# First chunk of a two-layer encoder: raw weights with a place for each k-tile, token-major squares, 32-column float32 gates

## Chip, cores and metric

The kernel runs on one core of one Trainium2 chip. The metric is the device time of one execution in microseconds, as the median of several runs.

## What is computed

The reference is a two-layer encoder trunk on 256 tokens of width 2048, all in float32. Layer 0 mixes tokens with a bidirectional mLSTM (8 heads), layer 1 with a bidirectional gated recurrence (16 heads); each mixer and each gated MLP (width 5504) is preceded by an RMSNorm and added to the residual. Only the first projection concerns us:

```python
def rmsnorm(x, g):
    xf = x.astype(jnp.float32)
    xf = xf * lax.rsqrt(jnp.mean(xf * xf, axis=-1, keepdims=True) + EPS)
    return xf.astype(x.dtype) * g

def mlstm_mixer(hn, w_in, b_gate, head_g, w_out):
    p = hn @ w_in
    q, k, v, o, gates = jnp.split(p, [A_QK, 2 * A_QK, 2 * A_QK + A_V, 2 * A_QK + 2 * A_V], axis=-1)
    gates = (gates + b_gate).astype(jnp.float32).reshape(b, s, 4, A_HEADS)
    ...
```

There are 32 gate columns (4 kinds x 8 heads). `w_in` is 2048 x 6176, and about 440 MB of weights go through the core in one execution.

## The kernel before

**Products.** Weights and activations are each split into two parts of type float32r, a rounded high part and the rest: `wh` and `wl` for weights, the two halves of `xt` for x. A product is high by high plus the two mixed terms. ScalarE casts (`wh`, line 154, and `xt`, line 226), VectorE subtracts (`wl`, line 155, and `xt`, line 227). The activations are multiplied by the norm's gain `g` while they are split; the factor 1/rms of each token is multiplied in only when a product leaves PSUM, through `R` (a row for each token) or `rc` (a column).

**Chunks.** All projections form one list of chunks, each 256 or 512 output columns over all k-tiles of 128 rows. `stream` walks through it. A generator, `split_weights`, loads raw weights (SP's queue, line 138, three buffers `raw` of 2048 columns), splits them in pieces of 1024 columns into `wh` and `wl` (four buffers each), and is asked for pieces three ahead of their use. In a chunk of kind "fm" (features on partitions) a k-tile takes lines 202 and 206; in one of kind "tm" (tokens on partitions) lines 215 to 217, twice. Each chunk holds PSUM banks, of which there are four for products, until its `done` function has emptied them. Other work (heads, norms, transposes) is put between the matmuls by the `Side` object's estimates of time. The order of each engine's instructions is finally set by a scheduler with a simulated time line; an instruction that is pinned (`tc.keep_in_program_order`) stays behind the instruction of its engine that the program has before it.

**The first chunk** is of a kind of its own, "first". It makes 512 columns of v and, in a third PSUM bank, the gates: 32 gate columns spread over 128 by zeros, so that each k-tile has 640 columns. Beside the six v matmuls a k-tile has two for the gates (lines 219, 220). Its raw weights go through the three `raw` buffers, k-tiles 0 to 3 one by one and then in pairs (`FIRST`). x arrives feature-major as `xT`, in the tile `gx`, with the gains in its first 16 columns: k-tiles 0 and 1 on ScalarE's queue (line 143), the others on SP's, each behind the raw weights of its k-tile (line 146). In the loop ScalarE also squares four k-tiles of x at a time (line 258), VectorE adds these up (line 262), and `pc` (line 269) sums over the features. From that `finish` makes `rc` and, with the matmul `pr` (line 308), `R`. Constants and parameters are loaded behind the tenth k-tile (line 242).

After the chunk, x is loaded again, token-major, over the place of `gx` (`hm`, the residual; line 602, GpSimd's queue). `gates` then makes the mLSTM's decay terms from the gate products (lines 435 to 482), while the second chunk (`w_aq[0]`: q) runs. Ahead of it all, 39 small matmuls on a tile of ones (`idle`, line 880) keep TensorE busy during the first loads.

Of the kernel before, what the change touches and what calls it, by code (L numbers as in the profile page):

```python
# [8 lines left out]
F32 = mybir.dt.float32  # L9
F32R = mybir.dt.float32r  # L10
# [5 lines left out]
P = 128  # L16
T = 256
# [29 lines left out]
FIRST = (0, 1, 2, 3, 4, 6, 8, 10, 12, 14, 16)  # L47
# [4 lines left out]
C_ID, C_MF, C_MB, C_LV = 0, 128, 384, 640  # L52
# [3 lines left out]
def trunk_kernel(ctx, tc, xT, x_d, fg_d, pp_d, cst_d, w_first, w_aq, w_ak, w_av, w_ao, w_aout,  # L56
# [15 lines left out]
    gx = keep.tile([P, KT + KT * T], F32, name="gx")  # L72
    hx = gx[:, KT:].rearrange("p (k t) -> p k t", k=KT)
    hT = [hx[:, k] for k in range(KT)]
    hm = hx.rearrange("p k t -> p (k t)").rearrange("p (a c) -> p a c", a=2)
# [41 lines left out]
    class Chunk:  # L117
        def __init__(self, kind, src, nk, x, done, before=None, last=False, swap=()):
            self.last, self.swap = last, swap
            self.kind, self.src, self.nk, self.x, self.done, self.before = kind, src, nk, x, done, before  # L120
            self.width = {"fm": 256, "tm": 512, "first": 512 + P}[kind]

    def split_weights(chunks):

        first = True
        for ch in chunks:
            total = ch.nk * ch.width
            cuts = [0]
            if first:
                cuts = [k * ch.width for k in FIRST]  # L130
            while cuts[-1] < total:
                cuts.append(min(total, cuts[-1] + 2048))
            step = ch.width if first else 1024
            for b0, b1 in zip(cuts, cuts[1:]):
                n = b1 - b0
                raw = wpool.tile([P, 2048], F32, tag="raw", bufs=RAW, name="raw")
                pin = tc.keep_in_program_order if first else lambda ins: ins
                pin(nc.sync.dma_start(raw[:, :n], ch.src[:, b0:b0 + n]))
                if first:
                    k0, k1 = b0 // ch.width, b1 // ch.width  # L140
                    if k0 == 0:
                        for a, b in ((0, KT + T), (KT + T, KT + 2 * T)):
                            nc.scalar.dma_start(gx[:, a:b], xT[:, a:b])
                    elif k0 > 1:
                        a, b = KT + k0 * T, KT + k1 * T
                        pin(nc.sync.dma_start(gx[:, a:b], xT[:, a:b]))
                for c0 in range(0, n, step):
                    m = min(step, n - c0)
                    wh = wpool.tile([P, 1024], F32R, tag="wh", bufs=WB, name="wh")
                    wl = wpool.tile([P, 1024], F32R, tag="wl", bufs=WB, name="wl")  # L150
                    r = raw[:, c0:c0 + m]
                    if first and b0 == 0:
                        ch.x(0, pin)
                    pin(act.copy(wh[:, :m], r))  # L154
                    pin(dve.tensor_tensor(wl[:, :m], r, wh[:, :m].bitcast(F32), ALU.subtract))  # L155
                    if first and b0:
                        ch.x((b0 + c0) // ch.width, pin)
                    yield wh, wl, m // ch.width
            first = False

    def stream(chunks):
# [10 lines left out]
        for ch in chunks:  # L172
            if ch.before:
                ch.before()
            ps = [psm.tile([P, 512], F32, tag="mm", name="mm") for _ in range(3 if ch.kind == "first" else 2)]
            k = 0
            while k < ch.nk:
# [31 lines left out]
                for kk in range(n):  # L209
                    x = ch.x(k)  # L210
                    st, sp = k == 0, k == ch.nk - 1
                    c = slice(kk * 512, (kk + 1) * 512)
                    for t in range(2):
                        xh, xl = x[:, t * P:(t + 1) * P], x[:, T + t * P:T + (t + 1) * P]
                        pe.matmul(ps[t], xh, wh[:, c], start=st, stop=False)  # L215
                        pe.matmul(ps[t], xh, wl[:, c], start=False, stop=False)  # L216
                        pe.matmul(ps[t], xl, wh[:, c], start=False, stop=sp)  # L217
                    if ch.kind == "first":
                        pe.matmul(ps[2], wh[:, 512:512 + P], x, start=st, stop=False)
                        pe.matmul(ps[2][:, 0:T], wl[:, 512:512 + P], x[:, 0:T], start=False, stop=sp)  # L220
                    side.tick(1.3)
                    k += 1
# [22 lines left out]
    class Norm:  # L245
# [5 lines left out]
        def take(self, k, src, *pin):  # L251
            self.xs[k] = keep.tile([P, 2 * T], F32R, tag=f"xt{k}", name=f"xt{k}")
            split(self.xs[k], src, gx[:, k:k + 1] if pin else col(self.g, self.o + k), *pin)

        def squares(self, i, mp, pin):

            s = mp.tile([P, 4 * T], F32, tag="sq4", bufs=2, name="sq4")
            pin(act.activation(s, hx[:, 4 * i:4 * i + 4].rearrange("p a b -> p (a b)"), AF.Square))
            if i == 0:
                self.acc4 = s  # L260
                return
            pin(dve.tensor_tensor(self.acc4, self.acc4, s, ALU.add))
            if i == 3:
                a = self.acc4
                dve.tensor_tensor(a[:, 0:2 * T], a[:, 0:2 * T], a[:, 2 * T:4 * T], ALU.add)
                dve.tensor_tensor(a[:, 0:T], a[:, 0:T], a[:, T:2 * T], ALU.add)
                pc = [aux("pc") for _ in range(2)]
                for t in range(2):
                    pe.matmul(pc[t][:, 0:1], a[:, t * P:(t + 1) * P], ones[:, 0:1], start=True, stop=True)
                self.finish([pc[t][:, 0:1] for t in range(2)])  # L270

        def add(self, c):

            if c == 0:
                self.ss = ev.tile([P, 2, 4], F32, tag="ss8", bufs=2, name="ss8")
            cs = slice(512 * c, 512 * c + 512)
            for t in range(2):
                square(hm[:, t, cs], self.ss[:, t, c:c + 1])
            side.push(self.turn(c))

        def turn(self, c):
# [10 lines left out]
            if c == 3:  # L292
                ss = self.ss
                dve.tensor_tensor(ss[:, :, 0:2], ss[:, :, 0:2], ss[:, :, 2:4], ALU.add)
                dve.tensor_tensor(ss[:, :, 0:1], ss[:, :, 0:1], ss[:, :, 1:2], ALU.add)
                self.finish([ss[:, t, 0:1] for t in range(2)])

        def finish(self, sums):
# [75 lines left out]
    def square(src, total):  # L374
        jk = ev.tile([P, 512], F32, tag="jk", bufs=1, name="jk")
        act.activation(jk, src, AF.Square, accum_out=total)
# [27 lines left out]
    def mlstm(norm, nxt):  # L404
# [3 lines left out]
        cp = tc.tile_pool(name="cols", bufs=1)  # L408
        box = {}

        def first_x(k, pin=None):
            if pin is None:
                return norm.xs[k]
            norm.take(k, hT[k], pin)
            if k in (5, 9, 12, 15):
                if k == 5:
                    box["sp"] = startup.enter_context(tc.tile_pool(name="sp", bufs=1))
                norm.squares((5, 9, 12, 15).index(k), box["sp"], pin)
                if k == 15:
                    startup.close()  # L420
            if k == 10:
                late(cst[:, 0:C_LV], cst_d[:, 0:C_LV])
                late(pp, pp_d)

        def begin():
            c = stack.enter_context(cp)
# [142 lines left out]
        for pr in range(AH // 2):  # L569
# [27 lines left out]

            def done_first(ps, done_v=done_v):
                done_v(ps[0:2])
                gates(ps[2])  # L600
                for t in range(2):
                    pool.dma_start(hm[:, t], x_d[t])

            if pr == 0:
                chunks.append(Chunk("first", w_first, KT, first_x, done_first, begin))
            else:
                chunks.append(Chunk("tm", w_av[pr - 1], KT, norm.x, done_v))
# [270 lines left out]
    for i in range(39):  # L878
        o = i % 4 * QUAD
        pe.matmul(idle[o:o + QUAD, 0:120], ones[:, 0:QUAD], ones[:, 0:120], start=True, stop=True)  # L880
# [31 lines left out]
def _constants():  # L912
    c = np.zeros((P, NCST), np.float32)
    s, t = np.arange(P)[:, None], np.arange(P)[None, :]
    c[:, C_ID:C_ID + P] = s == t
    c[:, C_MF:C_MF + P] = np.where(s > t, BIG, 0.0)
# [7 lines left out]
def layout(x, norm_mix_g, norm_ffn_g, mlstm_w_in, mlstm_b_gate, mlstm_head_g, mlstm_w_out, hgrn_w_in, hgrn_lb,  # L924
# [3 lines left out]
    wg = np.zeros((D, P), np.float32)  # L928
    bg = np.zeros((P, 1), np.float32)
    for i, r in enumerate((0, 64, 32, 96)):  # L930
        wg[:, r:r + AH] = wa[:, 6144 + i * AH:6144 + (i + 1) * AH]
# [12 lines left out]
        w_first=np.concatenate([wa[:, 2048:2560].reshape(KT, P, 512), wg.reshape(KT, P, P)], axis=2)  # L944
        .transpose(1, 0, 2).reshape(P, KT * (512 + P)),
# [11 lines left out]
def build(nc, ins, out_shape=(2, P, D), **kw):  # L957
# [4 lines left out]
    with tile.TileContext(nc, schedule_with_timeline_sim=True) as tc:  # L962
        with ExitStack() as ctx:
            trunk_kernel(ctx, tc, ap["xT"], ap["x"], ap["fg"], ap["pp"], ap["cst"], ap["w_first"],
# [15 lines left out]
```

## Time and profile before

| | us |
|---|---|
| median of 3 runs (2418.76 to 2421.82) | 2419.44 |
| the profiled execution | 2421.37 |
| its span | 2419.6 |
| TensorE busy | 2406.7 |
| VectorE busy | 1694.1 |
| ScalarE busy | 1221.1 |

The profile is of one execution. The span is the time from its first to its last instruction; the profiled execution's own time has a little beside it. Busy times of an engine overlap those of the others, and matmuls are pipelined, so that the sum of their lengths says less than the distance between their starts. The granted TensorE clock was 0.999 over the span.

### The profile page before, as it was taken

How to read it: one execution, taken by the hardware profiler on the slowest of the kernel's cores; microseconds unless marked ns; L12 is line 12 of the kernel's file. 1: busy time of each engine (PE TensorE's matmuls, PEld its weight loads, DVE VectorE, ACT ScalarE, POOL GpSimd, SP SyncE). 2: the span in 40 equal slices, each digit the busy share in tenths (PEclk: the TensorE clock that was granted, in tenths of full speed). 3: DMA queues.
4: the chain of work that ended last, by engine and by line, in shares of the span. 5: the costliest groups of instructions: out<-in, count | busy, mean ns of one | idle time of the engine just before them, and what ended most of it. 6: DMA issues, size and time to landing. Idle time of an engine off the chain costs nothing.

```text
span 2419.6 us, 36956 instructions
## 1 busy us (share of the span) xinstructions
PE 2406.7 (99%) x14646; PEld 2060.3 (85%) x14646; DVE 1694.1 (70%) x2784; ACT 1221.1 (50%) x1879; POOL 161.7 (7%) x223
## 2 busy tenths in 40 slices
PE   9999999999999999999999999999999999999998
PEld 7888888888888888888888888888888888888887
DVE  7766656777645777656898989885777754677754
ACT  6655455444434445445555555555544443444443
POOL 0100000000000000001222222220000000000000
PEclk9999999999999999999999999999999999999999
DMA  8654555555555555555545554555555555555554
GB/s 290 200 182 162 186 176 189 190 188 189 181 196 201 188 187 189 192 185 183 173 173 175 175 175 167 168 185 190 183 191 190 192 188 195 194 190 192 192 188 142
DMA packets 66925, 451.90 MB, mean 187 GB/s; under 512 B 7600, under 2 KB 8368, under 8 KB 14144
## 3 DMA queue, kind: packets, MB, share of 16 engines
q1 hardware_dynamic: 64656, 442.92, 54.0%
q0 software_dynamic: 1232, 5.31, 0.9%
q8 instruction: 114, 1.87, 0.3%
q10 hardware_dynamic: 864, 1.32, 0.2%
q14 instruction: 59, 0.48, 0.1%
HBM read 447.35 MB, written 2.16 MB: 186 GB/s over the span
## 4 chain that ended last, share of the span: by engine, by line
PE 98%; DMA 1%; DVE 0%; issue 0%; ACT 0%; SPq 0%; POOLq 0%; POOL 0%; DVEq 0%
PE mm L202 36%; PE mm L206 18%; PE mm L215 13%; PE mm L216 13%; PE mm L217 13%; DMA gx<-in_xT 1%; PE pn L533 1%; PE py L763 1%; PE pd L713 0%; PE pz L288 0%; PE pa L713 0%; PE S L519 0%; PE pz L784 0%; PE pa L738 0%; PE pa L737 0%
## 5 line engine op out<-in xcount | busy, mean ns | idle before, releaser
L155 DVE TENSOR_TENSOR wl<-raw,wh 128x1024 fp32r<-128x1024 f32 (+1 forms) x848 | 1031.9, 1218 | 582.3 <-ACT wh L154 572.4
L202 PE MATMUL mm<-xt,wh 128*128 128x512 f32 x3776 | 1315.6, 394 | 0.0
L154 ACT CAST wh<-raw 128x1024 fp32r<-128x1024 f32 (+1 forms) x848 | 881.2, 1041 | 859.0 <-PE mm L217 400.9
L206 PE MATMUL mm<-xt,wl 128*128 128x256 f32 x3776 | 1048.8, 278 | 0.0
L202 PEld LDWEIGHTS mm<-xt,wh 128*128 128x128 f32 x3776 | 707.0, 188 | 160.7
L206 PEld LDWEIGHTS mm<-xt,wl 128*128 128x128 f32 x3776 | 710.0, 188 | 3.2 <-DVE wl L155 0.3
L217 PE MATMUL mm<-wh,g 128*128 128x512 f32 x674 | 262.8, 390 | 0.0
L215 PE MATMUL mm<-wh,g 128*128 128x512 f32 x674 | 262.5, 390 | 0.0
L216 PE MATMUL mm<-wl,g 128*128 128x512 f32 x674 | 262.3, 389 | 0.0
L215 PE MATMUL mm<-wh,xt 128*128 128x512 f32 x512 | 198.9, 393 | 2.9 <-ACT xt L226 2.1
L216 PE MATMUL mm<-wl,xt 128*128 128x512 f32 x512 | 198.5, 392 | 0.2 <-DVE wl L155 0.2
L217 PE MATMUL mm<-wh,xt 128*128 128x512 f32 x512 | 198.0, 391 | 0.0
L231 ACT COPY b<-mm 128x256 f32<-128x256 f32 x237 | 87.6, 369 | 166.6 <-PE mm L206 166.5
L217 PEld LDWEIGHTS mm<-wh,g 128*128 128x128 f32 x674 | 126.5, 188 | 26.5
L215 PEld LDWEIGHTS mm<-wh,g 128*128 128x128 f32 x674 | 126.5, 188 | 26.4
L216 PEld LDWEIGHTS mm<-wl,g 128*128 128x128 f32 x674 | 126.5, 188 | 25.8
L215 PEld LDWEIGHTS mm<-wh,xt 128*128 128x128 f32 x512 | 95.1, 188 | 23.2 <-ACT xt L226 3.3
L217 PEld LDWEIGHTS mm<-wh,xt 128*128 128x128 f32 x512 | 96.1, 188 | 20.0 <-DVE xt L227 0.4
L216 PEld LDWEIGHTS mm<-wl,xt 128*128 128x128 f32 x512 | 96.1, 188 | 19.9 <-DVE wl L155 1.2
L232 DVE TENSOR_TENSOR a<-mm,b 128x256 f32<-128x256 f32 x86 | 36.5, 424 | 52.2 <-ACT b L231 52.2
L705 DVE COPY kq<-QK 128x256 f32<-128x256 f32 x224 | 69.6, 335 | 0.0
L731 POOL TENSOR_TENSOR G<-G 128x384 f32<-128x384 f32 (+2 forms) x96 | 67.8, 706 | 6.3
(206 smaller groups left out, 1836.7 us busy)
## 6 DMA issues: line engine op xcount, KB each, us to landing
raw<-in_w_up SPq DMA_DIRECT2D x172, 1024.0 KB, 5.0
raw<-in_w_down SPq DMA_DIRECT2D x80, 1024.0 KB, 4.8
raw<-in_w_bq SPq DMA_DIRECT2D x48, 1024.0 KB, 5.0
raw<-in_w_ao SPq DMA_DIRECT2D x16, 1024.0 KB, 4.8
raw<-in_w_aout SPq DMA_DIRECT2D x16, 1024.0 KB, 4.7
raw<-in_w_bv SPq DMA_DIRECT2D x16, 1024.0 KB, 4.7
raw<-in_w_bg SPq DMA_DIRECT2D x16, 1024.0 KB, 4.7
raw<-in_w_bout SPq DMA_DIRECT2D x16, 1024.0 KB, 4.8
```

Source lines behind the costliest of these rows:

```text
L154: pin(act.copy(wh[:, :m], r))
L155: pin(dve.tensor_tensor(wl[:, :m], r, wh[:, :m].bitcast(F32), ALU.subtract))
L202: pe.matmul(ps[f], wh[:, c:c + P], x, start=k + kk == 0, stop=False)
L206: pe.matmul(ps[f][:, 0:T], wl[:, c:c + P], x[:, 0:T], start=False, stop=k + kk == ch.nk - 1)
L215: pe.matmul(ps[t], xh, wh[:, c], start=st, stop=False)
L216: pe.matmul(ps[t], xh, wl[:, c], start=False, stop=False)
L217: pe.matmul(ps[t], xl, wh[:, c], start=False, stop=sp)
L231: act.copy(b, ps[:, T:2 * T])
L232: dve.tensor_tensor(dst, ps[:, 0:T], b, ALU.add)
L533: pe.matmul(pn[:, 0:258], w, v, start=(i == 0), stop=(i == len(parts) - 1))
L705: dve.tensor_copy(m[:, j].rearrange("k (m p j) -> k m p j", p=2, j=h), blocks(z, h, 0, T))
L731: pool.tensor_tensor(G2, G[:, 0:6 * n:2], G[:, 1:6 * n:2], ALU.mult)
```

## The change

In the first chunk:

- Raw weights: each of the 16 k-tiles has a place of its own (the tiles `yt0` to `yt15`, not otherwise used until later), and `load` issues all their transfers at the start, with x between them; each is 128 x 512 (256 KB). Behind them on SP's queue come the gate weights, the first half of the next raw weights, x token-major (`hm`, now a tile of its own), the other half, constants and parameters.
- The gates leave the k loop. Their 32 columns are multiplied by the gains in float32 (`gate`, one VectorE instruction). After the loop 16 float32 matmuls, each 32 columns wide, read x as it was loaded; four run in the four column groups, each group adding up four k-tiles in PSUM (`pq`). A matmul with a 0/1 matrix (`C_SUM`, `pg`) adds the four groups and puts the rows where `gates` wants them.
- The chunk is of kind "tm", with two PSUM banks. Its first k-tile has the products in the order high-high, low-x, low-w.
- Sums of squares come from `hm`: eight ScalarE instructions with an accumulated sum (`squares`) and two small additions (`total`), pinned behind the split of the second chunk's first piece. `squares` is the function that the later norms use. The squares of feature-major x, their sums and `pc` are gone.
- `gx` and the gate weights lie in a pool that is closed after the gate products; `begin` (the mLSTM's tiles) is called after that.
- 40 idle matmuls instead of 39.

The core of the diff:

```diff
     def split_weights(chunks):
-            if first:
-                cuts = [k * ch.width for k in FIRST]
...
+        first, loaded = chunks[0], []
+        raws = first.load(loaded, chunks[1])
+        for k in range(KT):
+            if k == 0:
+                first.x(0, pin)
+            wh, wl = parts(raws[k], 512, pin)
+            if k:
+                first.x(k, pin)
+            yield wh, wl, 1
+        for ch in chunks[1:]:
             total = ch.nk * ch.width
+            for b0 in range(0, total, 2048):
+                b1 = min(total, b0 + 2048)
+                raw = loaded.pop(0) if loaded else load_raw(ch.src, b0, b1)
+                for c0 in range(0, b1 - b0, 1024):
+                    m = min(1024, b1 - b0 - c0)
+                    if ch is chunks[1] and b0 == c0 == 0:
+                        first.gate()
+                        wh, wl = parts(raw[:, c0:c0 + m], m, pin)
+                        first.sums()
+                    else:
+                        wh, wl = parts(raw[:, c0:c0 + m], m)
                     yield wh, wl, m // ch.width
...
-                    if ch.kind == "first":
-                        pe.matmul(ps[2], wh[:, 512:512 + P], x, start=st, stop=False)
-                        pe.matmul(ps[2][:, 0:T], wl[:, 512:512 + P], x[:, 0:T], start=False, stop=sp)
+                    ops = [(t, i) for t in range(2) for i in range(3)]
+                    if ch.first and st:
+                        ops.sort(key=lambda o: (0, 2, 1)[o[1]])
...
+        def load(loaded, follower):
+            raws = [keep.tile([P, 512], F32, tag=f"yt{k}", name=f"raw{k}") for k in range(KT)]
+            def w(k):
+                pin(nc.sync.dma_start(raws[k], w_first[:, k * 512:(k + 1) * 512]))
+            def x(q, a, b):
+                q.dma_start(gx[:, a:b], xT[:, a:b])
+            x(nc.scalar, 0, KT + T)
+            x(nc.scalar, KT + T, KT + 2 * T)
+            w(0)
+            w(1)
+            for k in range(2, KT, 2):
+                pin(nc.sync.dma_start(gx[:, KT + k * T:KT + (k + 2) * T], xT[:, KT + k * T:KT + (k + 2) * T]))
+                w(k)
+                w(k + 1)
+            late(wg, w_gate)
+            r = wpool.tile([P, 2048], F32, tag="raw", bufs=RAW, name="raw")
+            loaded.append(r)
+            late(r[:, 0:1024], follower.src[:, 0:1024])
+            for c in range(2):
+                for t in range(2):
+                    late(hm[:, t, c * 1024:(c + 1) * 1024], x_d[t, :, c * 1024:(c + 1) * 1024])
+            late(r[:, 1024:2048], follower.src[:, 1024:2048])
+            late(cst[:, 0:C_LV], cst_d[:, 0:C_LV])
+            late(pp, pp_d)
+            return raws
...
-        def gates(ps):
+        def gates(gs):
...
-                fm_scaled(ps, R, gz)
+                pg = aux("pg")
+                pe.matmul(pg[:, 0:T], cst[:, C_SUM:C_SUM + P], gs, start=True, stop=True)
+                dve.tensor_tensor(gz, pg[:, 0:T], R, ALU.mult)
...
+            def gate():
+                pin(dve.tensor_tensor(gw, gw, gx[:, 0:KT].unsqueeze(2).broadcast_to([P, KT, GATES]), ALU.mult))
+            def sums():
+                for c in range(4):
+                    norm.squares(c, pin)
+                norm.total(pin)
             def done_first(ps, done_v=done_v):
-                done_v(ps[0:2])
-                gates(ps[2])
-                for t in range(2):
-                    pool.dma_start(hm[:, t], x_d[t])
+                pq = aux("pq")
+                for k in range(KT):
+                    o = k % 4 * GATES
+                    pin(pe.matmul(pq[o:o + GATES, 0:T], gw[:, k], hx[:, k], start=k < 4, stop=k >= KT - 4))
+                gs = ev.tile([P, T], F32, tag="b", bufs=3, name="gs")
+                act.copy(gs, pq[:, 0:T])
+                startup.close()
+                begin()
+                norm.finish()
+                done_v(ps)
+                gates(gs)
...
-    for i in range(39):
+    for i in range(40):
```

More of the change, by code (lines that the diff above doesn't have):

```diff
@@ L46 @@
 LEAD = 48
-FIRST = (0, 1, 2, 3, 4, 6, 8, 10, 12, 14, 16)
+GATES = 4 * AH
 QUAD = 32
@@ L71, in trunk_kernel @@
     hmx = keep.tile([P, 2], F32, name="mhalf")
[L72 to L75, printed above, removed]
+    hm = keep.tile([P, 2, D], F32, name="hm")
     ident = cst[:, C_ID:C_ID + P]
@@ L117, in trunk_kernel, with __init__ @@
     class Chunk:
-        def __init__(self, kind, src, nk, x, done, before=None, last=False, swap=()):
-            self.last, self.swap = last, swap
+        def __init__(self, kind, src, nk, x, done, before=None, last=False, swap=(), first=False):
+            self.last, self.swap, self.first = last, swap, first
             self.kind, self.src, self.nk, self.x, self.done, self.before = kind, src, nk, x, done, before
-            self.width = {"fm": 256, "tm": 512, "first": 512 + P}[kind]
-    def split_weights(chunks):
-        first = True
-        for ch in chunks:
-            total = ch.nk * ch.width
-            cuts = [0]
-            if first:
-                cuts = [k * ch.width for k in FIRST]
[L131 to L157, printed above, removed]
@@ L174, in stream @@
                 ch.before()
-            ps = [psm.tile([P, 512], F32, tag="mm", name="mm") for _ in range(3 if ch.kind == "first" else 2)]
+            ps = [psm.tile([P, 512], F32, tag="mm", name="mm") for _ in range(2)]
             k = 0
@@ L249, in __init__, with take, squares @@
             self.xs, self.done = [None] * KT, False
-        def take(self, k, src, *pin):
+        def take(self, k, src, g=None, *pin):
             self.xs[k] = keep.tile([P, 2 * T], F32R, tag=f"xt{k}", name=f"xt{k}")
[L253 to L272, printed above, removed]
+            split(self.xs[k], src, col(self.g, self.o + k) if g is None else g, *pin)
+        def squares(self, c, pin=lambda ins: ins):
             if c == 0:
@@ L292, in turn, with finish @@
             if c == 3:
[L293 to L298, printed above, removed]
+                self.total()
+                self.finish()
+        def finish(self):
+            sums = [self.ss[:, t, 0:1] for t in range(2)]
             self.rc_ = ev.tile([P, 2], F32, tag="rc", bufs=2, name="rc")
@@ L407, in mlstm @@
         stack, startup = ExitStack(), ExitStack()
-        cp = tc.tile_pool(name="cols", bufs=1)
-        box = {}
-        def first_x(k, pin=None):
[L412 to L423, printed above, removed]
+        sp = startup.enter_context(tc.tile_pool(name="sp", bufs=1))
```

60 lines of the change are left out of this document (42 added, 18 removed).

## The prediction

> **What bounds the kernel now.** I read the page first (span, busy time, the chain), then who waited for whom, then the first 40 us in order of time, since the edit lies there.
>
> ```profile
> span 2419.6 us, 36956 instructions
> PE 2406.7 (99%) x14646; PEld 2060.3 (85%) x14646; DVE 1694.1 (70%) x2784; ACT 1221.1 (50%) x1879; POOL 161.7 (7%) x223
> PE 98%; DMA 1%; DVE 0%; issue 0%; ACT 0%; SPq 0%; POOLq 0%; POOL 0%; DVEq 0%
> ```
> TensorE is the bound, and the chain that ended last is its matmuls. The waits of TensorE over the whole span are four (us in total, times, longest):
>
> ```profile
> PE mm L215 <- ACT xt L226: 2.1, 3, 0.8
> PE idle L880 <- POOL ones L873: 1.1, 1, 1.1
> PE mm L215 <- ACT wh L154: 0.8, 1, 0.8
> PE mm L216 <- DVE wl L155: 0.2, 1, 0.2
> ```
> All four belong to the first chunk or lie before it; afterwards TensorE never waits. So whatever brings the first matmul of the second chunk forward should bring the end forward by as much, if the second chunk then finds its data. The first chunk in order of time (start, length, engine, line; in brackets the idle time before and what ended it):
>
> ```profile
> 5.67 0.73 PE L215 MATMUL mm<-wh,xt 128*128 128x512 f32 x2 [0.80 <-ACT wh L154]
> ...
> 16.73 0.63 PE L215 MATMUL mm<-wh,xt 128*128 128x512 f32 x2
> ...
> 18.12 0.39 PE L219 MATMUL mm<-xt,wh 128*128 128x512 f32 x1
> 18.46 0.63 PE L215 MATMUL mm<-wh,xt 128*128 128x512 f32 x2
> ...
> 27.16 0.63 PE L215 MATMUL mm<-wh,xt 128*128 128x512 f32 x2
> ...
> 37.73 0.40 PE L202 MATMUL mm<-xt,wh 128*128 128x512 f32 x1
> 38.08 0.40 PE L202 MATMUL mm<-xt,wh 128*128 128x512 f32 x1
> ```
> It lasts from 5.67 to 37.73, 32.06 us for 16 k-tiles. Undisturbed, from 16.73 to 27.16, six k-tiles take 10.43 us, 1.74 each, of which the two gate matmuls (L219 to the next L215) take 18.46 - 18.12 = 0.34 and the six of v the other 1.40. 16 x 1.74 = 27.8, so 4.2 us are stalls. The chain says what they wait for: x, issued late and landing slowly (start, length).
>
> ```profile
> 6.87 4.55 DMA gx<-in_xT
> 19.51 9.82 DMA gx<-in_xT
> ```
> And who holds the issue back is the queue's own wait for one of three raw buffers:
>
> ```profile
> SPq L138 <- DVE wl L155: 20.2, 8, 6.6
> ```
>
> **The change part by part.** Gate matmuls out of the k loop: -16 x 0.34 = -5.4 us of TensorE, all on the path.
>
> Stalls: with a place for each k-tile nothing waits for a buffer. The first tile's own ramp stays (0.2 us; its order now puts the xl products ahead of the wl ones, which suits the later wl), the first cast is 512 columns instead of 640 and lets TensorE start 0.1 earlier. So -4.0 - 0.1 = -4.1. What could be late next is the split of each k-tile and the transfers. The split:
>
> ```profile
> L155 DVE TENSOR_TENSOR wl<-raw,wh 128x640 fp32r<-128x640 f32 (+1 forms) x17 | 14.2, 843 | 6.0 <-ACT wh L154 4.3 <-PE mm L220 1.6
> L154 ACT CAST wh<-raw 128x640 fp32r<-128x640 f32 (+1 forms) x18 | 13.3, 752 | 5.9 <-DMA raw<-in_w_first 5.9
> L226 ACT ACTIVATE xt<-gx 128x256 fp32r<-128x256 f32 x15 | 7.6, 506 | 3.4 <-DMA gx<-in_xT 3.4
> L227 DVE SCALAR_TENSOR_TENSOR xt<-gx,xt 128x256 fp32r<-128x256 f32 x15 | 7.2, 478 | 2.7 <-ACT xt L226 2.7
> ```
> Even for 640 columns ScalarE needs at most 0.75 + 0.51 = 1.26 and VectorE 0.84 + 0.48 = 1.32 us a k-tile, under 1.40; 512 columns take less. Covered. (Groups of 5.6 to 37.7 us: busy, mean ns of one, idle before them.)
>
> The transfers: a k-tile is now 128 x 512 x 4 = 262 KB of weights and 131 KB of x, 0.393 MB. The rate in slices of 1 us over the first 40:
>
> ```profile
> GB/s 0 33 183 375 375 382 36 74 321 297 277 315 360 358 332 352 339 262 344 377 352 247 391 411 421 434 438 419 434 425 408 217 25 90 172 393 426 401 369 311
> raw<-in_w_first SPq DMA_DIRECT2D x6, 640.0 KB, 7.0
> raw<-in_w_first SPq DMA_DIRECT2D x4, 320.0 KB, 3.9
> ```
> At 3 to 6 us, when only the first transfers of 320 and 128 KB are in flight, it is 375 to 382; at 8 to 20 it is 262 to 377; at 22 to 30 it is 391 to 438. I take 350 for the short rows of the first chunk and 410 behind it, flowing from 3.0 us. A k-tile then lands every 1.12 us, so the transfers run ahead of TensorE; the sixteenth (6.30 MB) lands at 3.0 + 18.0 = 21.0, and is wanted at about 26.
>
> First chunk's end: 5.6 + 0.2 + 16 x 1.40 = 28.2.
>
> The 16 gate products are new: float32, 32 columns wide, 256 moving, four column groups. They are put on TensorE behind the first chunk, with nothing to hide them. Near rows, where float32 products show as two instructions each:
>
> ```profile
> 1.09 3.77 PE L880 MATMUL idle<-ones 128*32 128x120 f32 x78 [1.09 <-POOL ones L873]
> 1165.81 0.87 PE L713 MATMUL pd<-kq 128*32 128x32 f32 x78
> 46.12 0.60 PE L308 MATMUL pr<-dg,ones 128*128 128x128 f32 x4
> 41.04 0.50 PE L269 MATMUL pc<-ones,sq 128*128 128x1 f32 x4
> ```
> L308: four instructions in 0.60 us, 0.27 of it the last one's length, 0.11 per 128 columns, so 0.22 per 256. If four groups run beside each other, 32 instructions take 8 x 0.22 = 1.8. By columns, 32 x 256 = 8192 at the pace of L880 (9360 in 3.77) would take 3.3, at L713's (2496 in 0.87) 2.9; the floor is the 1.40 / 6 = 0.23 us for 512 columns of the v matmuls, shared by four, 0.9. I take 1.8, from the row whose instructions are nearest in length; ends 0.9 and 3.3. So the second chunk can start at 28.2 + 1.8 = 30.0 instead of 37.73, 7.7 us sooner.
>
> Sum of squares: the pc matmuls (0.50) go, the gate sum pg of 256 columns comes, priced as the four of L308 (0.60): +0.1. Off TensorE, the four wide squares and three adds of the first chunk go; eight squares from token-major x come, on ScalarE's queue behind the cast of the second chunk's first piece, and wait for hm. Queued behind them is the cast of that chunk's second piece.
>
> ```profile
> L376 ACT ACTIVATE jk<-gx x32: 622/632/635, 331.5 to 2412.0; 128x512 f32<-128x512 f32 x32
> L376 ACT ACTIVATION_READ_ACCUMULATOR jk<-gx x32: 185/187/189, 332.0 to 2412.5; 128x1 f32 x32
> 34.75 1.99 ACT L154 CAST wh<-raw 128x1024 fp32r<-128x1024 f32 x2
> 36.52 1.21 DVE L155 TENSOR_TENSOR wl<-raw,wh 128x1024 fp32r<-128x1024 f32 x1
> ```
> The four wh buffers let the first piece's cast start when TensorE has done its 13th k-tile, 5.8 + 13 x 1.40 = 24.0; it ends at 25.0, eight squares of 0.63 to 0.82 end at 30.0 to 31.6, the second piece's cast at 31.0 to 32.6, its wl at 32.2 to 33.8. TensorE wants them after eight pairs of 0.35 (38.08 - 37.73), at 30.0 + 2.8 = 32.8 and 33.0. So the wait here lies between 0 and about 0.8.
>
> The queue of SP, in order: gate weights 0.262 MB, half of the next raw 0.524, hm 2.097, the other half 0.524, constants 0.393, parameters 0.242, then the second raw of that chunk, 1.049. Gate weights land at 3.0 + 6.56 / 0.350 = 21.7, hm 2.62 MB later at 28.1 (the last two squares want it at about 30), the second raw, 4.83 MB later, at 33.5. TensorE wants that raw's first piece at 30.0 + 5.6 = 35.6, the cast takes 1.0, so landed by 34.6: 1.1 us to spare. For these two places I charge 0.8 us, ends 0 and 3.
>
> The sums are then ready before the second chunk is well under way, R comes sooner within it than now, and hm no longer loads through Pool. The tiles that take over the place of gx are first written in the second chunk, behind the gate products that read it; TensorE wants none of them before the heads.
>
> Sum: -5.4 - 4.1 + 1.8 + 0.1 + 0.8 = -6.8. The profiled execution took 2421.37 (1.8 beside the span), so 2414.6; it lies 1.9 above the median of the runs, 2419.44, so the median becomes 2412.6.
>
> [...] In this trace small transfers reach 375 GB/s while several are in flight. [...]
>
> **The rivals.** First, the transfers are a little too slow and the gain is given back in the second chunk. 11.39 MB must land by 34.6. At 330 GB/s they land at 37.5, 2.9 late: gain 4.7, 2414.7; at 300 at 41.0, 6.4 late: gain 1.2, 2418.2. For it: the slices at 8 to 20 average about 330. Against: there the issues came in bursts, and the longer rows behind run at over 400.
>
> Second, parts that do not do what they say: gate products one after the other instead of four at once, 32 x 0.22 = 7.0, gain 7.6 - 5.2 = 2.4, less the wait of 0.8, 2417.8 (against: L880 and L713, far above that pace per instruction column); or SP is still held back, by something other than buffers, and the stalls of 4.0 stay: gain 7.6 - 4.0 - 0.8 = 2.8, 2416.6.
>
> Third, slower: short transfers do not reach their rate however many are queued, and everything of the second chunk lies behind hm and constants in one queue. Below 11.39 / (34.6 + 7.6 - 3.0) = 291 GB/s more is lost than won. The nearest row of a low rate (its last three columns: granted clock, share of the DMA engines, GB/s):
>
> ```profile
> 5.67:10.00 4.33, 4.33 (x19) 3.39 (x20) 3.07 (x5) 2.33 (x5) 0.00 (x0) 1.00 0.66 195
> ```
> At 195 the second raw lands at 61.4, 26.8 late, less 7.6: 19 us slower, 2438.6. Against: in that stretch the engines were busy for 0.66 only, because SP waited for buffers.
>
> **How the numbers follow.** 0.2% is 4.8 us, about what a measurement of this kernel can tell from no change. Forecast, a gain of 4.8 to 8.6: 0.73. First rival beyond 4.8: 0.12. Second: 0.05. Third: 0.08. The other 0.02 is a gain of over 8.6. So faster 0.75, same 0.17, slower 0.08. The range: at the low end products at 0.9, no wait and nothing else, 2412.6 - 0.9 - 0.8 = 2410.9, with 0.9 for the scatter of medians 2410.0; at the high end the first rival at 300 GB/s, 2418.2. Left out are the third rival and small parts of the others.
>
> **What would show it.** Right: L215 steps of 1.40 without stalls, the last v matmul by 28.5, gate products in 1.5 to 2.5 us, the first fm matmul near 30, SP issuing x and the first weights without a pause for a buffer, no later wait above 1 us. Wrong: waits of TensorE for wh or wl of the second chunk (first or third rival, by the rate in the slices), gate products of 7 us, or waits later in the kernel where there are none now.

## The result, and the profile after

| | before | after |
|---|---|---|
| median of 18 runs (us) | 2419.56 | 2414.75 |
| lowest to highest | 2418.76 to 2421.82 | 2414.36 to 2416.29 |
| profiled execution | 2421.37 | 2416.08 |
| its span | 2419.6 | 2414.3 |

The ratio is 0.9979, with a 95% interval of 0.9972 to 0.9986: 4.8 us, or 0.2%, faster. The forecast was 2412.6, in a range of 2410.0 to 2418.2.

The page of the changed kernel:

```profile
span 2414.3 us, 36960 instructions
PE 2403.0 (100%) x14646; PEld 2056.9 (85%) x14646; DVE 1688.4 (70%) x2781; ACT 1221.2 (51%) x1891; POOL 159.7 (7%) x221
```

Who waited for whom, TensorE, whole span (us in total, times, longest):

```profile
PE idle L910 <- POOL ones L903: 1.1, 1, 1.1
PE mm L205 <- DVE wl L133: 0.7, 2, 0.5
PE mm L201 <- ACT wh L132: 0.6, 1, 0.6
```

TensorE in order of time (lines of the new kernel: 217 is v, 201 and 205 are the second chunk's high and low weights, 624 the gate products):

```profile
5.27 1.55 PE L217 MATMUL mm<-wh,xt 128*128 128x512 f32 x4
...
10.32 0.62 PE L217 MATMUL mm<-wl,xt 128*128 128x512 f32 x2
...
11.68 0.62 PE L217 MATMUL mm<-wl,xt 128*128 128x512 f32 x2
...
27.64 0.61 PE L201 MATMUL mm<-xt,wh 128*128 128x512 f32 x2
28.19 1.93 PE L624 MATMUL pq<-gx,wg 128*32 128x256 f32 x32
30.05 0.50 PE L205 MATMUL mm<-xt,wl 128*128 128x256 f32 x2
...
36.48 0.73 PE L201 MATMUL mm<-xt,wh 128*128 128x512 f32 x2 [0.61 <-ACT wh L132]
37.74 0.51 PE L205 MATMUL mm<-xt,wl 128*128 128x256 f32 x2 [0.53 <-DVE wl L133]
...
55.20 0.40 PE L217 MATMUL mm<-wh,xt 128*128 128x512 f32 x1
```

The waits of the first chunk are gone: v takes from 5.27 to 27.64, 1.40 a k-tile in the mean (the first k-tiles take longer; the undisturbed step is 1.36, as from 10.32 to 11.68). The gate products hold TensorE from 28.19 to 30.05. New are waits in the second chunk, nearly all for the split of its third piece. The fourth chunk starts at 55.20; in the trace of before it starts at 61.17:

```profile
61.17 0.40 PE L215 MATMUL mm<-wh,xt 128*128 128x512 f32 x1
```
So 6.0 us are won by there, of which 5.3 remain at the end of the span. 0.3 are lost in layer 1's gated recurrence and 0.2 at the very end; the rest is scattered.

This profiled execution lies 1.3 above its median. A second one, of the same kernel (below, called the typical one), took 2414.48. There the waits shrink to this:

```profile
PE idle L910 <- POOL ones L903: 1.1, 1, 1.1
PE mm L205 <- DVE wl L133: 0.5, 1, 0.5
```

The GB/s in slices of 1 us over the first 40 us, first profile and typical one:

```profile
GB/s 0 45 207 366 300 328 350 412 391 410 395 383 389 391 379 381 383 371 385 363 276 285 385 356 369 414 369 406 405 431 443 421 434 410 385 393 418 229 82 0
```
```profile
GB/s 0 43 177 371 319 330 348 402 410 399 389 381 387 391 391 383 385 385 389 397 401 418 406 418 406 410 414 395 443 437 413 426 451 369 369 410 188 82 8 188
```

They differ at 20 to 24 us: 276, 285, 385, 356, 369 against 401 to 418. The second chunk's second raw is issued at 24.0 in the one and 23.0 in the other, and the fourth chunk starts 1.5 us apart (55.20, 53.73).

### The profile page after: what moved, and what is told of

The parts are those of the page before. It is cut to its first block, busy times and chain, and to the rows that moved or that the text cites. A ratio compares the mean times of both kernels' runs of the same rounds, so it can differ in the third digit from the quotient of the medians.

```text
span 2414.3 us, 36960 instructions
## 1 busy us (share of the span) xinstructions
PE 2403.0 (100%) x14646; PEld 2056.9 (85%) x14646; DVE 1688.4 (70%) x2781; ACT 1221.2 (51%) x1891; POOL 159.7 (7%) x221
## 4 chain that ended last, share of the span: by engine, by line
PE 98%; DMA 1%; ACT 0%; issue 0%; SPq 0%; DVE 0%; POOLq 0%; POOL 0%; ACTq 0%
PE mm L217 40%; PE mm L201 36%; PE mm L205 18%; PE pn L547 1%; PE py L793 1%; DMA raw<-in_w_first 1%; PE pd L743 0%; PE pz L276 0%; PE pa L743 0%; DMA raw<-in_w_aq 0%; PE S L533 0%; DMA gx<-in_xT 0%; ACT jk L363 0%; PE pz L814 0%; PE pa L768 0%
## 5 line engine op out<-in xcount | busy, mean ns | idle before, releaser
L217 PE MATMUL mm<-wh,g 128*128 128x512 f32 x1348 | 416.6, 390 | 0.0
L217 PE MATMUL mm<-wh,xt 128*128 128x512 f32 x1024 | 319.8, 391 | 0.0
L217 PE MATMUL mm<-wh,yb 128*128 128x512 f32 x256 | 80.7, 393 | 0.0
L217 PE MATMUL mm<-wh,ya 128*128 128x512 f32 x256 | 80.5, 393 | 0.0
L755 DVE TENSOR_TENSOR QK<-QK,G 128x256 f32<-128x256 f32 x112 | 56.9, 513 | 0.0
```

Of the source, the lines that this page charges most:

```text
L217: pe.matmul(ps[t], x[:, a + t * P:a + (t + 1) * P], w[:, c], start=st and i == 0, stop=sp and i == 2)
L755: dve.tensor_tensor(ka, ka, gview(G, n, 1, h), ALU.mult)
```

## The experiments

Every kernel was timed against runs of the kernel before on the same chip. e1 to e4 ran on one chip, e5 to e11 on another, e12 on a third; the medians of before beside them lie between 2419.59 and 2420.70, so a difference of some tenths between rows of different chips says little. "Start of the fourth chunk" is the first tm matmul behind q and k in each trace.

| kernel | median (us) | ratio to before, 95% | start of fourth chunk |
|---|---|---|---|
| change | 2414.75 | 0.9972 to 0.9986 | 55.20 |
| e1, second cast pinned | 2415.17 | 0.9971 to 0.9990 | 54.61 |
| e2, raw ahead of hm | 2414.07 | 0.9967 to 0.9986 | 52.75 |
| e3, four gate products | 2414.77 | 0.9967 to 0.9987 | 53.62 |
| e4, ring of three | 2419.45 | 0.9985 to 1.0005 | 58.58 |
| e5, change again | 2414.70 | 0.9971 to 0.9989 | 53.73 |
| e6, raw ahead of hm again | 2413.83 | 0.9966 to 0.9985 | 53.37 |
| e7, feature-major squares | 2421.83 | 1.0000 to 1.0017 | 61.97 |
| e8, order of queue only | 2414.60 | 0.9969 to 0.9987 | 52.89 |
| e9, places alone | 2416.88 | 0.9979 to 0.9997 | 56.78 |
| e10, feature-major squares, hm last | 2414.03 | 0.9968 to 0.9986 | 53.75 |
| e11, e6 with four gate products | 2412.56 | 0.9959 to 0.9981 | 52.01 |
| e12, before again | 2420.88 | 0.9993 to 1.0011 | 61.14 |

### e1: the second cast pinned behind the squares

```diff
                         first.sums()
+                    elif ch is chunks[1] and b0 == 0:
+                        wh, wl = parts(raw[:, c0:c0 + m], m, pin)
```

> The cast of the second chunk's second piece is pinned behind all eight squares, instead of standing between the third and the fourth; transfers are as in the change. Theory A (the second raw of that chunk lands too late, at about 34.6 us, and its split takes 2.3 us more): the squares end near 31 instead of 35.3 and the cast of the third piece starts when the raw has landed, near 34.7 instead of 35.4, so only some 0.7 us of the wait of about 2 us goes: 2414.75 becomes 2414.0. Rival B (ScalarE's order is the whole cause: a cast that waits for a transfer holds back five squares that could run): the wait goes altogether, 2412.7.

2415.17 (2414.25 to 2416.06, in two groups of five): no gain that the times could show, so theory A's 2414.0 was missed as well. The profiled execution (2415.72) has the same dip in the rate as the change's first (260 and 277 GB/s at 20 to 22 us); against that one its fourth chunk starts 0.6 sooner, near theory A's 0.7, and 0.4 are left at the end. The waits stay, earlier by a piece:

```profile
33.07 0.73 PE L203 MATMUL mm<-xt,wh 128*128 128x512 f32 x2 [0.16 <-ACT wh L132]
34.33 0.50 PE L207 MATMUL mm<-xt,wl 128*128 128x256 f32 x2 [0.53 <-DVE wl L133]
```
Rival B alone (2412.7) is out. The order on ScalarE is not the whole cause: putting the cast last only moved the wait to the second piece.

### e2 and e6: the second raw ahead of token-major x

```diff
             late(r[:, 0:1024], follower.src[:, 0:1024])
+            late(r[:, 1024:2048], follower.src[:, 1024:2048])
+            r2 = wpool.tile([P, 2048], F32, tag="raw", bufs=RAW, name="raw")
+            loaded.append(r2)
+            late(r2, follower.src[:, 2048:4096])
             for c in range(2):
                 for t in range(2):
                     late(hm[:, t, c * 1024:(c + 1) * 1024], x_d[t, :, c * 1024:(c + 1) * 1024])
-            late(r[:, 1024:2048], follower.src[:, 1024:2048])
```

with the first three pieces of the second chunk pinned and `first.sums()` behind the third.

> The second raw of the second chunk is issued ahead of token-major x instead of behind it, the constants and the parameters, and the squares come behind that raw's first piece on ScalarE. Theory A: the raw lands near 28, the third piece is split before 31, TensorE waits for nothing in the second chunk and the 2 us come back: about 2412.7. Sums are ready near 36, still ahead of the third chunk, which wants the first chunk's PSUM banks near 41. Rival B gives the same only if the squares no longer stand ahead of a cast; under rival C (the later squares make R, rc and so the third chunk late) a new wait of 1 to 3 us shows near 41: 2414 to 2416.

> The kernel with the second raw ahead of token-major x and the squares behind that raw's first piece, once more, against the change on one chip: 0.7 to 1.0 us below the change (2413.7 to 2414.1 against 2414.7), as there is no wait left in its second chunk; 0 if the earlier difference was scatter.

2414.07 and 2413.83: 0.7 to 0.9 below the change, both times. TensorE's waits, e6:

```profile
PE idle L913 <- POOL ones L906: 1.1, 1, 1.1
PE mm L217 <- ACT xt L223: 0.3, 1, 0.3
PE mm L217 <- ACT wh L132: 0.2, 1, 0.2
```
None is in the second chunk, as theory A says; but these kernels change the order on ScalarE along with that of the queue. The 2 us I expected back were read from the change's first profile; the typical execution loses only 0.8 there, and that is what comes back (0.87 between e5 and e6, on one chip). Rival C (a wait near 41) did not show. This is the best of the kernels run that compute everything.

### e3 and e11: twelve gate products left out

```diff
-                for k in range(KT):
+                for k in range(4):
                     o = k % 4 * GATES
-                    pin(pe.matmul(pq[o:o + GATES, 0:T], gw[:, k], hx[:, k], start=k < 4, stop=k >= KT - 4))
+                    pin(pe.matmul(pq[o:o + GATES, 0:T], gw[:, k], hx[:, k], start=True, stop=True))
```

in the change (e3) and in e2's kernel (e11).

> Twelve of the 16 gate products are left out (the gates are then wrong), so TensorE reaches the second chunk 1.4 us sooner. Theory A: the third piece's data come as late as before, the wait there grows by what is saved: no gain, 2414.6 to 2414.8. Rival B, if ScalarE waits for the gate products nowhere: the same as A, since its squares do not move. Rival D (matmul time alone sets the end, the waits are constant): 1.4 us less, 2413.3.

> The kernel with the second raw ahead of token-major x, with twelve of the 16 gate products left out (the gates are then wrong). Where the same omission from the change saved nothing, here nothing waits in the second chunk, so theory A gives the full 1.3 us: about 2412.5 against 2413.8. If it again saves nothing, something other than the second chunk's data sets the pace behind the first chunk.

Both kernels so leave out three quarters of the sums for the gates. From the change the omission took nothing: 2414.77 against 2414.75, so rival D (2413.3) is out. TensorE came sooner and waited longer:

```profile
28.52 0.64 PE L624 MATMUL pq<-gx,wg 128*32 128x256 f32 x8
...
35.15 0.73 PE L201 MATMUL mm<-xt,wh 128*128 128x512 f32 x2 [0.66 <-ACT wh L132]
36.41 0.50 PE L205 MATMUL mm<-xt,wl 128*128 128x256 f32 x2 [0.53 <-DVE wl L133]
```
From the kernel without that wait it took 1.27 us (2413.83 to 2412.56). So in the change the second chunk's data, and not TensorE, set the time at that place; with the orders of e2, TensorE does.

### e4: the places undone

The first chunk's raw weights go through `raw` again (k-tiles 0 to 3, then pairs), each with its x behind it:

```diff
-        raws = first.load(loaded, chunks[1])
-        for k in range(KT):
+        for k0, k1 in zip(FIRST, FIRST[1:]):
+            raw = first.load(k0, k1)
+            if k1 == KT:
+                first.rest(loaded, chunks[1])
```

> Only the places are undone: the first chunk's raw weights go through the three raw buffers, one by one and then in pairs, with x behind them, as before the change; gates apart and token-major squares stay. If the places brought the 4 us of stalls: the k-tile steps are 1.36 us with stalls of 4 to 6 us between them, and everything behind in the queue comes later, so 4 to 8 us are lost: 2418.8 to 2422. Rival E (a quarter fewer bytes in the first chunk remove the stalls anyway): v ends within 1 us of the change and the time is 2414.8 to 2416.

2419.45, within what was expected: 4.7 above the change and not to be told from the kernel before (0.9985 to 1.0005), though gates and squares are those of the change. Its waits on TensorE:

```profile
14.32 0.73 PE L221 MATMUL mm<-wh,xt 128*128 128x512 f32 x2 [2.58 <-ACT xt L227]
...
36.18 0.73 PE L205 MATMUL mm<-xt,wh 128*128 128x512 f32 x2 [0.41 <-ACT wh L133]
37.44 0.50 PE L209 MATMUL mm<-xt,wl 128*128 128x256 f32 x2 [0.53 <-DVE wl L134]
...
42.23 0.50 PE L209 MATMUL mm<-xt,wl 128*128 128x256 f32 x2 [0.52 <-DVE wl L134]
```
v ends 3.1 us later than in the change (30.78), and the second chunk waits as well. Rival E is out: without the places, the shorter k-tile of the gates apart brings nothing that these times can show.

### e9: the places alone

On the kernel before, gates and squares as they were; the three `raw` buffers hold three k-tiles each, filled as soon as they are free:

```diff
+                    for g in ((0, 3, 6) if k == 0 else (k + 6,) if k % 3 == 0 and k + 6 < KT else ()):
+                        places[g] = wpool.tile([P, 2048], F32, tag="raw", bufs=RAW, name="raw")
+                        for kk in range(g, min(g + 3, KT)):
...
+                            o = (kk - g) * ch.width
+                            pin(nc.sync.dma_start(places[g][:, o:o + ch.width], ch.src[:, kk * ch.width:(kk + 1) * ch.width]))
```

> The kernel before with only the places changed: nine k-tiles of raw weights (640 columns each, gates in the loop as before) are in flight ahead of use instead of three, x between them; squares, gates and everything behind stay as before. Theory G (the stalls are the larger part of what the change gained, because a shorter k-tile alone only waits longer): k-tiles of 1.74 us without stalls, the first chunk ends near 33.4 instead of 37.7, 4.3 us less: 2415.3. Rival H (the prediction's shares: stalls 4.1, gates 3.6 net, and only 1 to 2 us lost behind): the same 2415.3, but then the change should lie 2 us or more below this kernel; under G it lies within 1 us of it.

2416.88, in a narrow band (2416.67 to 2417.34). The trace shows just what was expected, 16 steps without a stall, the last beginning at 31.86 and ending 1.73 later, at 33.6 instead of 37.7:

```profile
5.67 0.73 PE L223 MATMUL mm<-wh,xt 128*128 128x512 f32 x2 [1.08 <-ACT wh L162]
...
31.86 0.63 PE L223 MATMUL mm<-wh,xt 128*128 128x512 f32 x2
```
Against the profiled execution of before it is 4.5 us better, against the medians of before on the same chip (2419.73) 2.85. The 2415.3 that both theories gave was missed by 1.6: the 4.3 were read from a profiled execution and taken off a median. Two things follow. The change lies 2.1 below this kernel, which fits rival H and not G: places and gates apart each bring a part, but the second part shows only on top of the first (e4). And before's distance from its own profile to its median probably lies in what the places remove, see below.

### e7 and e10: feature-major squares

```diff
+                if k in (5, 9, 12, 15):
+                    norm.squares4((5, 9, 12, 15).index(k), hx, sp, pin)
...
-                norm.finish()
+                norm.finish(norm.sums4())
...
+                for t in range(2):
+                    pool.dma_start(hm[:, t], x_d[t])
```

In e10 `hm` is loaded by SP, behind the second raw, instead of these last two lines.

> Only the squares are undone: squares of feature-major x in the first chunk (four of 1024 columns), summed by the two pc matmuls; token-major x is loaded behind the first chunk by GpSimd's queue, as before the change. Theory A: 2.1 MB less stand ahead of the second raw, it lands about 5 us sooner, no wait in the second chunk; pc costs 0.4: 2414.0 to 2414.4. If token-major squares themselves brought time (rival F), this is slower than the change by 0.5 us or more.

> The squares undone once more (feature-major x, pc matmuls), now with token-major x pinned last in SP's queue, behind the second raw, so that it can't start ahead of the first weights. Theory A (what stands ahead of the second raw counts, not the squares as such): no wait in the second chunk, pc costs 0.4 us more on TensorE: 2414.0 to 2414.4. Rival F (token-major squares themselves bring time, because four squares of 1024 columns in the loop hold up the casts): waits in the first chunk, 2415.5 or more.

e7 missed by 7 us, and not because of the squares. `hm` is now a tile of its own, so nothing held GpSimd's load of it back, and it started at 1.3 us, behind the weights of the first two k-tiles only (0.73) and ahead of the third's (2.1). GpSimd, then ScalarE and TensorE, in e7:

```profile
1.32 1.24 POOL L649 DMA_DIRECT2D hm<-in_x  x2 [0.21 <-issue]
```
```profile
13.66 0.62 ACT L132 CAST wh<-raw 128x512 fp32r<-128x512 f32 x1 [7.25 <-DMA raw<-in_w_first]
14.74 1.22 PE L217 MATMUL mm<-wh,xt 128*128 128x512 f32 x2 [5.84 <-ACT xt L223]
```
The third k-tile's weights, issued by SP at 2.1, had landed only by 13.66. Behind the wait the granted clock was lower for a time (busy time by stretches; the last three columns are granted clock, share of the DMA engines, GB/s):

```profile
9.00:14.00 5.00, 0.00 (x0) 0.00 (x0) 0.00 (x0) 0.34 (x1) 0.00 (x0) 0.92 1.01 399
14.00:16.60 2.60, 1.86 (x4) 1.49 (x5) 2.29 (x5) 2.60 (x7) 0.00 (x0) 0.50 1.06 391
16.60:19.20 2.60, 2.60 (x8) 2.01 (x7) 1.95 (x5) 2.60 (x6) 0.00 (x0) 0.50 1.06 389
19.20:22.00 2.80, 2.80 (x12) 2.27 (x11) 2.02 (x4) 1.65 (x4) 0.00 (x0) 0.86 1.05 386
```
After TensorE had stood still for 5.8 us, the granted clock was 0.50 for about its next 5 us of work. In e12, below, it was 0.50 for some 3 us, and there the longest wait was 1.4 us. What sets the clock is not shown by these runs.

With `hm` last in SP's queue, e10 took 2414.03, inside what theory A gave. So token-major squares as such bring nothing beyond the 0.2 us to e6; rival F is out. What counts is what stands ahead of the second chunk's weights in the queue.

### e8: the order of the queue alone

e2's edit of `load`, with the squares left where the change has them.

> Only the order of SP's queue is changed (second raw ahead of token-major x); the squares stay behind the first piece on ScalarE. Theory A alone: as good as with the squares moved, 2413.7 to 2414.1. Rival B (casts stand behind squares that wait for token-major x, which now lands about 2.5 us later): the third piece's cast waits for the squares, the wait is 1.5 to 3 us, and the time 2414.7 to 2416.5.

2414.60, as the change, 0.8 above e6, and between what theory A (up to 2414.1) and rival B (from 2414.7) gave. In the trace the second chunk has no wait (fourth chunk at 52.89, as early as in e2), so the time is not lost where rival B has it. But the scheduler had moved the casts, which are not pinned: the third piece's stands behind one square here, behind all eight in the change (34.20, see e5). So the order on ScalarE changed with that of the queue, and rival B's wait had no occasion to come. What was won is given back later, mostly in a wait that the change does not have:

```profile
28.51 1.03 ACT L132 CAST wh<-raw 128x1024 fp32r<-128x1024 f32 x1
```
```profile
81.19 0.52 PE L550 MATMUL pn<-Vh,Wl 128*128 128x258 f32 x2 [0.52 <-DVE Wl L542]
```
From the start of the fourth chunk to the first residual add 269.7 us pass here, against 269.2 in e6. Theory A is right that the wait goes and was too narrow as to the end. The other 0.3 of the 0.8 is not explained.

### e5 and e12: change and before once more

> The changed kernel itself, for a second profile and more times. Its first profile took 2416.08, 1.3 above the median of its runs, and its transfer rate fell to about 280 GB/s at 20 to 22 us, where another kernel's stayed near 400. If the wait in the second chunk is set by the transfers (theory A), an execution near the median shows no such dip, the second raw lands about 1.2 us sooner and the wait there is about 1 us instead of 2. If it is set by the order on ScalarE alone, the wait stays 2 us.

The execution near the median has no dip in the rate and a wait of about 0.8, as theory A has it. TensorE there, then ScalarE (the second piece's cast, then the third's and fourth's), then the second raw:

```profile
35.41 0.63 PE L201 MATMUL mm<-xt,wh 128*128 128x512 f32 x2
36.54 0.50 PE L205 MATMUL mm<-xt,wl 128*128 128x256 f32 x2 [0.50 <-DVE wl L133]
36.88 0.39 PE L201 MATMUL mm<-xt,wh 128*128 128x512 f32 x1
```
```profile
29.47 1.04 ACT L132 CAST wh<-raw 128x1024 fp32r<-128x1024 f32 x1 [2.36 <-DMA raw<-in_w_aq]
...
34.20 1.99 ACT L132 CAST wh<-raw 128x1024 fp32r<-128x1024 f32 x2
```
```profile
23.01 0.33 SPq L124 DMA_DIRECT2D raw<-in_w_aq  x1
raw<-in_w_aq SPq DMA_DIRECT2D x1, 1024.0 KB, 10.4
```
The second raw landed at 33.4 (issued 23.0, 10.4 to landing); ScalarE, which had waited 2.4 us for the first raw's other half with five squares still to do, reached it at 34.2. So what came last here was ScalarE, and not the landing that theory A names. But ScalarE had been held up by the other half, which stands behind `hm` in the queue: the queue's order acts through both, and these runs do not part them.

> The kernel before itself, for a second profile. Its first profiled execution took 2421.37, in the upper part of its runs (2418.5 to 2422.0). Theory J (the 1.9 us by which that execution lay above the median were part of its first chunk's stalls, which the change removes, and not an offset that the change keeps): an execution near 2419.2 shows stalls of 2.0 to 2.5 us in the first chunk instead of 4.2, its second chunk starts near 35.6 instead of 37.7, and behind that the two executions run alike. Rival K (the 1.9 us lie elsewhere in the execution): the first chunk again ends near 37.7 and the difference shows later.

The profiled execution took 2421.30, in the upper part again, so theory J stays unproved. It differs from the first all the same: the long stall lies elsewhere, and the granted clock is 0.50 from about 14.6 to 18 us; the longest wait before that is 1.4.

```profile
12.79 0.50 PE L215 MATMUL mm<-wh,xt 128*128 128x512 f32 x1 [1.40 <-ACT xt L226]
...
35.70 0.63 PE L215 MATMUL mm<-wh,xt 128*128 128x512 f32 x2
```
```profile
14.00:15.00 1.00, 1.00 (x5) 0.83 (x4) 0.65 (x1) 0.88 (x3) 0.00 (x0) 0.79 1.06 327
15.00:16.60 1.60, 1.60 (x5) 1.25 (x5) 1.58 (x4) 1.60 (x3) 0.00 (x0) 0.50 0.98 386
16.60:18.30 1.70, 1.70 (x6) 1.34 (x5) 0.94 (x2) 1.70 (x4) 0.00 (x0) 0.59 0.90 266
```
Two executions of one kernel, each with some 4 us lost in the first chunk in another way (here by estimate 1.7 of them by the clock, half of the 3.4 us from 14.6 to 18 at 0.50), and equal to 0.1 us from the fourth chunk on (61.17 and 61.14).

## Why the prediction was right, and where it was not

**The bound.** As predicted, what the second chunk's start gains arrives at the end, but for some tenths: a lead of 6.0 at the fourth chunk and 5.3 at the end in the first profile, 7.4 and 6.9 in the typical execution. The sum put this loss of 0.5 to 0.7 at nothing.

**Gates out of the loop and stalls.** v without stalls at 1.40 a k-tile in the mean, as predicted. It ends at 27.6 to 27.8, not 28.2: the start came 0.3 to 0.4 sooner (0.1 was predicted) because x landed earlier too (4.20 and 4.31 instead of 4.49). e9 measures the stalls alone at 4.1 in the trace, the term of the sum.

**The gate products.** 1.86 us of TensorE, 1.8 predicted, from the row of `pr`. The ends of 0.9 and 3.3 were not needed, and the second rival (products one after the other) did not come.

**The second chunk.** A wait of 0.8 was charged; the typical execution has 0.8 (from 35.41 to 36.88 for two pairs that take 0.70), the first profile 2.1. That the size fits is luck, for it was charged mainly to the second piece and came at the third. The working had the second piece's cast behind all eight squares, which were to end by 31.6; in the trace it stands among them, and they end only at 34.2. The landing of the second raw, 33.5, was met at 33.4, by two errors that cancel: the rates were higher than assumed, but by then the slices add up to 12.3 MB and not 11.4, as the next chunk's weights, issued at 24.3, load beside it. And the working had a hole: I counted the cast (1.0) against the deadline and not the subtraction (1.2) that the low product needs right behind it, and called 1.1 us spare, nearly all of which was not there. The charge "ends 0 and 3" covered it.

**The median.** This is the step that failed: "it lies 1.9 above the median of the runs, 2419.44, so the median becomes 2412.6". The sum itself gave 2414.6 for the profiled execution, and the typical execution took 2414.48; that they agree so closely is in part luck, as the lead was 7.4 at the fourth chunk and 0.5 of it were lost behind. Taking off 1.9 assumed that the distance from profile to median is something the change keeps. The runs speak against it: over all its comparisons the kernel before spreads from 2418.5 to 2422.0; the one with only the stalls removed (e9) spreads from 2416.67 to 2417.34, the change from 2414.36 to 2416.46. In e9 the spread went with the stalls, though other kernels without them keep some (e2: 2413.44 to 2416.10). In medians, on the chip of e9, the places were worth 2.85 (2419.73 less 2416.88) and not the term's 4.1, and the rest of the change 2.1 and not 2.7. That makes 1.8 of the 2.1 us by which the forecast was too low; the other 0.3 lies between the two medians of before (2419.44 and 2419.73). That before's faster executions lose less in their first chunk is argued from the spreads, not seen: no profile of one was obtained, so the cause of the smaller term stays open. The gain of 4.8 lies on the lower edge of the stretch, 4.8 to 8.6, to which the forecast gave 0.73.

**The rivals.** Of the first (transfers a little slow, gain given back in the second chunk) the place was right and the cause not: 0.8 us were given back there, 2.1 in the first profile, though the rate in the typical execution was 378 to 388 with the short rows where I took 350. The third (short transfers never reach their rate, under 291 GB/s) did not come: the trace of the typical execution has 378 to 388 at 5 to 15 us, with the DMA engines busy throughout (shares of 1.03 and 1.06).

**"SP issues without a pause for a buffer"** was right by the letter. It paused for another reason, see the last section, but without the stalls that the second rival expected of that.

## To carry to other kernels

A stall that varies from run to run is a term with a spread: before adding a gain worked out from one profiled execution to a median, ask whether the distance between the two lies in the very part that the change removes. Here, fewer matmuls in a stage fed by transfers were worth nothing that could be told until the transfers were ahead (e4, 0.9985 to 1.0005 of before), and after that they were worth their full time only where the next stage's data were ahead too (e3, 0.02 us above the change, against e11, 1.27 below e6): order one queue by the time at which each piece is wanted, and count every step of a piece's preparation against its deadline. A tile that no longer shares its place with another loses a wait that may have kept its load in order (e7, where it started at 1.3 us).

## What the runs showed of the hardware that was not expected

In the typical execution of the change, SP's issues:

```profile
0.73 0.86 SPq L407 DMA_DIRECT2D raw<-in_w_first  x2
1.64 0.42 SPq L417 DMA_DIRECT2D gx<-in_xT  x1
2.11 0.91 SPq L407 DMA_DIRECT2D raw<-in_w_first  x2
3.06 0.44 SPq L417 DMA_DIRECT2D gx<-in_xT  x1
4.30 0.85 SPq L407 DMA_DIRECT2D raw<-in_w_first  x2
...
14.97 1.00 SPq L407 DMA_DIRECT2D raw<-in_w_first  x2
```
```profile
SPq L407 <- DMA gx<-in_xT: 2.3, 6, 0.8
```
With two of x on ScalarE's queue, eight transfers were under way by 3.5 us; the ninth was issued at 4.30, when the first of x had landed (issued at 0.73, 3.6 to landing), and from there on the issues wait for earlier transfers, though every tile has its own place. Whether the program or the queue sets that number, no run here shows. The last weights of the first chunk were issued at 15 to 16 us, not in one go. It cost nothing that these runs show, since the DMA engines stayed busy (shares of 1.03 and 1.06 at 5 to 15 us).

The same kernel's transfers fell to 276 GB/s for some us in one execution and not in another; what did that was not found.
